# A listed prologue and a modulation with stationary weights, in a two-layer hybrid mixer on one core

## The chip, the cores and the metric

The kernel runs on one core of a Trainium2 chip. The metric is the time of one execution on the device in microseconds; the time given is the median of several runs.

## The reference, cut to what matters

Two layers work on 1024 latent tokens and 256 context tokens of 1024 channels. Each layer begins with a modulated norm, then one input projection, three head groups (Fourier mixing, pooling, differential attention), gates, an output projection and a gated residual. The diff touches only the beginning of the first layer:

```
shift, scale, gate     = split(silu(c)     @ w_mod + b_mod, 3)
shift_c, scale_c, gate_c = split(silu(c_ctx) @ w_mod + b_mod, 3)
h  = rms_norm(x,   norm_g) * (1 + scale)   + shift
hc = rms_norm(ctx, norm_g) * (1 + scale_c) + shift_c
p  = h @ w_in          # and hc @ w_in
```

`shift` and `scale` have one value for each of the 1024 channels, for the latent tokens and for the context.

## The kernel before, in words

Each engine carries out its instructions in the order in which the program lists them. Transfers are queued on SP, in their listed order too; a tile of a pool waits for a free buffer. The pool `big` (tag `t5`) has 28 buffers, PSUM 8 banks (`PX`) in this phase.

*Layout.* Tokens come in ten tiles `xn[0]` to `xn[9]` of 128 tokens (8 latent, 2 context), in three groups `g`: tiles 0 to 3, 4 to 7, 8 and 9. Channels come in eight tiles `k` of 128. The projection wants the channels on the partitions: `h_block(l, k, g, ...)` transposes the tiles of a group for channel tile k on TensorE (L280), multiplies by the scale and adds the shift out of PSUM (L284 on ScalarE or L286 on VectorE), copies that into a rounded part (L287, ScalarE) and subtracts to get the remainder (L289, POOL, for group 2 VectorE). `proj_T_k` (L340) then runs, for each of two output halves, three matmuls (rounded by rounded, remainder by rounded, rounded by remainder) into one PSUM bank for each half and group (`psg`). The split of a weight chunk into its two parts is `w_split` (L317, L318).

*Modulation.* Shift and scale of layer 0 come in four quarters of two channel tiles each. A quarter's weights are four transfers of 512 KB (`mod0_load`, L147). For quarters 0 to 2 `mod0_mm` (L156) holds `sc[:, k, :]` (128x2, silu of the two conditioning vectors) stationary and streams 512 columns of weights; the 2x512 result is copied to a row (L161), transposed in four pieces (L165) and finished by four small VectorE operations (`mod_finish`, L135 to L140). Quarter 3 is multiplied and accumulated on VectorE (`mod0_acc`, L175 and L177, 32 operations of 256 columns), summed over the partitions on TensorE (`mod0_sum`, L186, eight matmuls) and finished likewise.

*Norm.* `rms` squares a tile in two halves on ScalarE (L266) and takes three small POOL operations for the reciprocal root (L267 to L269); `norm` multiplies on VectorE (L581).

*Order.* The queue on SP carries quarters 0 to 2, the first weight chunk (two transfers of 512 KB), ten token tiles, quarter 3 and the next chunk. TensorE does the three quarters, then a loop over 24 items (k, g), first k = 0 to 5 for group 0, 1, 2, then k = 6 and 7, for which quarter 3 is needed. Item n's `hb` is listed before the matmuls `gk` of item n - 3; norms, the eight steps `next(acc)` of quarter 3 and its sum hang on chosen items.

Of the kernel before, what the change touches and what calls it, by code (L numbers as in the profile page):

```python
# [18 lines left out]
D = 1024  # L19
# [12 lines left out]
def build(tc, I, out):  # L32
# [13 lines left out]
    def nm(s):  # L46
        cnt[0] += 1
        return f"{s}_{cnt[0]}"
# [4 lines left out]
    def E2(shape=(128, 512), dt=F32):  # L53
        return e2p.tile(list(shape), dt, tag="e2", name=nm("e2"))

    def SM(n=1, dt=F32):
        return smp.tile([128, n], dt, tag=f"sm{n}", name=nm("sm"), bufs={1: 16, 4: 14}.get(n, 4))
# [9 lines left out]
    def PX(dt=F32, n=512):  # L67
        return PSP["pool"].tile([128, n], dt, tag="x", name=nm("x"))
# [60 lines left out]
    def mod_finish(l, k, sh, scl):  # L129

        n = sh.shape[1]

        def cols(t, o):
            return t[:, l, o + k:o + k + n].unsqueeze(2).to_broadcast([128, n, 2])
        dve.tensor_tensor(shiftT[l][:, k:k + n, :], sh, cols(bmodT, 0), ADD)  # L135
        t = SM(16)
        tv = t.rearrange("p (k t) -> p k t", t=2)[:, 0:n, :]
        dve.tensor_tensor(tv, scl, cols(bmodT, 8), ADD)
        dve.tensor_scalar(tv, tv, 1.0, None, ADD)
        dve.tensor_tensor(scaleT[l][:, k:k + n, :], tv, cols(ngT, 0), MULT)  # L140
# [7 lines left out]
            ws.append(w)  # L148
        return ws

    def mod0_mm(ws, half_way=None):
        ps = PX()
        for k in range(KT):
            if k == KT // 2 and half_way:
                half_way()
            pe.matmul(ps[0:2, :], lhsT=sc[:, k, :], rhs=ws[k // 2][:, k % 2, :], start=(k == 0), stop=(k == KT - 1))  # L156
        return ps

    def mod0_fin(q, pm):
        row = E2()  # L160
        dve.tensor_copy(row[0:2, :], pm[0:2, :])  # L161
        ps = PX()
        psv = ps[:, 0:8].rearrange("p (i c t) -> p i c t", i=2, c=2)
        for i in range(4):
            pe.transpose(ps[:, 2 * i:2 * i + 2], row[0:2, i * 128:i * 128 + 128], ident[0:2, 0:2])  # L165
        mod_finish(0, 2 * q, psv[:, 0], psv[:, 1])

    def mod0_acc(ws, acc):
        for k in range(KT):
# [7 lines left out]
                        dve.scalar_tensor_tensor(a, w, sk, a, MULT, ADD)  # L177
            yield

    def mod0_sum(q, acc):  # L180
        ps = PX()
        psv = ps[:, 0:8].rearrange("p (i c t) -> p i c t", i=2, c=2)
        for i in range(2):
            for ct in range(2):
                for t in range(2):
                    pe.matmul(psv[:, i, ct, t:t + 1], lhsT=acc[:, 2 * i + t, ct * 128:ct * 128 + 128],  # L186
                              rhs=ones[:, 0:1], start=True, stop=True)
        mod_finish(0, 2 * q, psv[:, 0], psv[:, 1])

    def mod_acc(src, c0, sides, res, lead=1):  # L190

# [67 lines left out]
    def x_rms(x, r):  # L259

        ss = SM(2)
        for hf in range(2):
            if hf:
                yield
            sq = E2()
            act.activation(sq, x[:, hf * 512:hf * 512 + 512], AF.Square, accum_out=ss[:, hf:hf + 1])  # L266
        pool.tensor_tensor(r, ss[:, 0:1], ss[:, 1:2], ADD)  # L267
        pool.tensor_scalar(r, r, 1.0 / D, EPS, MULT, ADD)
        pool.tensor_tensor(r, r, mhalf[:, 0:1], ALU.pow)  # L269

    GROUPS = {0: (0, 1, 2, 3), 1: (4, 5, 6, 7), 2: (8, 9)}

    def h_block(l, k, g, xn, H, on_act=False):
        tiles = GROUPS[g]
        s = 1 if g == 2 else 0
        n = 128 * len(tiles)
        c0 = tiles[0] * 128
        ps = PX()
        for i, j in enumerate(tiles):
            pe.transpose(ps[:, i * 128:i * 128 + 128], xn[j][:, k * 128:k * 128 + 128], ident)  # L280
        hf = E2()
        sc1, sh1 = scaleT[l][:, k, s:s + 1], shiftT[l][:, k, s:s + 1]
        if on_act:
            act.activation(hf[:, :n], ps[:, :n], AF.Identity, scale=sc1, bias=sh1)  # L284
        else:
            dve.tensor_scalar(hf[:, :n], ps[:, :n], sc1, sh1, MULT, ADD)  # L286
        act.activation(H[k][0][:, c0:c0 + n], hf[:, :n], AF.Copy)  # L287
        eng = dve if g == 2 else pool
        eng.tensor_tensor(H[k][1][:, c0:c0 + n], hf[:, :n], H[k][0][:, c0:c0 + n].bitcast(F32), SUB)  # L289


    wsrc = []
# [245 lines left out]
    def layer(l, src, dst, carry):  # L538
# [23 lines left out]
        def newH(k):  # L562
            if H[k] is None:
                H[k] = [T5([128, NTOK], F32R) for _ in range(2)]

        if full:
            xn, rx = {}, {}

            def x_in(*js):
                for j in js:  # L570
                    xn[j] = x_load(src, j)

            def rms(*js):
                for j in js:
                    rx[j] = SM(1)
                    for _ in x_rms(xn[j], rx[j]):
                        pass

            def norm(*js):
                for j in js:  # L580
                    dve.tensor_scalar(xn[j], xn[j], rx[j], None, MULT)  # L581

            def hb(k, g, on_act):
                newH(k)
                h_block(l, k, g, xn, H, on_act)

            def gk(k, *gs):
                for ct in range(2):
                    proj_T_k(psg[ct], H, W, ct, ntokA, k, gs)

            wm = [mod0_load(q) for q in range(3)]
            w_dma()
            x_in(0, 1, 2, 3, 4, 5, 6, 7, 8, 9)
            ms = [mod0_mm(wm[0])]
            ms.append(mod0_mm(wm[1], lambda: mod0_fin(0, ms[0])))
            ms.append(mod0_mm(wm[2], lambda: mod0_fin(1, ms[1])))
            w_split()
            W = wready.pop(0)
            a3 = T5([128, 4, 256])
            psg = [[PX() for _ in cols(ntokA)] for _ in range(2)]  # L600
            items = [(k, g) for g in (0, 1, 2) for k in range(6)] + [(k, g) for k in (6, 7) for g in (0, 1, 2)]
            at = {n: [] for n in range(len(items))}
            at[0] += [lambda: rms(0, 1, 2, 3), lambda: norm(0, 1), lambda: mod0_fin(2, ms[2]), lambda: norm(2, 3)]
            for n, j in enumerate((4, 5, 6, 7, 8, 9)):
                at[n] += [lambda j=j: rms(j)]
                at[n + 1] += [lambda j=j: norm(j)]
            for n in range(8, 16):
                at[n] += [lambda: next(acc)]
            at[18] += [lambda: mod0_sum(3, a3)]
            for n in range(len(items) + 3):  # L610
                if n < len(items):
                    for f in at[n]:
                        f()
                    hb(*items[n], 6 <= n < 17)
                if n == 0:
                    w3 = mod0_load(3)
                    acc = mod0_acc(w3, a3)
                    w_dma()
                if n >= 3:
                    gk(*items[n - 3])  # L620
                if n == 20:
                    pool.tensor_scalar(pscT, pscT, 0.5, 0.0, MULT, ADD)
                    tabs = fourier_tabs(l)
                    css = [fourier_load(l, ct) for ct in range(2)]
                if n == 22:
                    w_split()
                    w_dma()
        else:
            xn, tail = carry
            k = 0  # L630
            for n in range(14):
                next(tail)
                if n in (4, 5, 6, 8, 9, 11, 12, 13):
                    newH(k)
                    h_block(l, k, 0, xn, H)
                    k += 1
            W = wready.pop(0)
            for k in range(k, KT):
                newH(k)
                h_block(l, k, 0, xn, H)  # L640
            psg = [[PX() for _ in cols(ntokA)] for _ in range(2)]
            hb = iter(range(KT))
            for k in range(KT):
                if k >= KT - 1:
                    h_block(l, next(hb), 1, xn, H)
                for ct in range(2):
                    proj_T_k(psg[ct], H, W, ct, ntokA, k, (0,))
                if k in (0, 1, 3, 7):
                    next(tail, None)
                if k == 1:  # L650
                    w_split()
                    w_dma()
                if k == 7:
                    css = [fourier_load(l, ct) for ct in range(2)]
            for k in range(-2, KT + 0):
                if (h := next(hb, None)) is not None:
                    h_block(l, h, 1, xn, H)
                if 0 <= k < KT:
                    for ct in range(2):
                        proj_T_k(psg[ct], H, W, ct, ntokA, k, (1,))  # L660
                if 0 <= k - 0 < KT:
                    h_block(l, k - 0, 2, xn, H)
# [698 lines left out]
```

## Time and profile before

| | us |
|---|---|
| median of 3 runs | 1412.21 (1408.42 to 1413.48) |
| the profiled execution's own time | 1411.95 |
| its span, first to last instruction | 1410.2 |
| TensorE busy in the span | 1345.6 (95%) |
| VectorE, POOL, ScalarE busy | 852.9, 799.1, 540.5 |

PE is TensorE's matmuls, PEld its weight loads, DVE VectorE, ACT ScalarE, POOL GpSimd, SP the queue of transfers. Times in rows are microseconds from the start of the span. A number with an x counts records; an f32 matmul leaves two records of each kind, a transpose one.

### The profile page before, as it was taken

The page shows a single profiled execution, that of the slowest core. Times are in us where ns is not written, and L with a number is a line of the kernel's source. Part 1 is how long each engine was busy: PE and PEld are TensorE (multiplying, and loading weights), DVE is VectorE, ACT ScalarE, POOL GpSimd, SP SyncE. Part 2 cuts the span into 40 slices and gives each one's busy share as a digit, 9 for nine tenths or more (in the row PEclk, how much of TensorE's full clock was granted, in tenths as well). Part 3 has the DMA queues.
Part 4 walks back from the last instruction along what each step waited for, and adds up shares of the span by engine and source line. Part 5 has one row for each costly group of instructions (what it writes and reads, how often), then busy time and mean ns, then how long its engine had stood idle before and what let it go on. Part 6 is the DMA issues. An engine that isn't in the chain of part 4 may idle for free.

```text
span 1410.2 us, 24603 instructions
## 1 busy us (share of the span) xinstructions
PE 1345.6 (95%) x9780; PEld 1206.5 (86%) x9780; DVE 852.9 (60%) x1274; ACT 540.5 (38%) x1152; POOL 799.1 (57%) x867
## 2 busy tenths in 40 slices
PE   7899999999999988999998899999999998899998
PEld 1688899889999977889997678898999996799997
DVE  2854366795975057677775554464365216878784
ACT  2632213111211156676664332221122216666662
POOL 2633216766574057788875732326676306777773
PEclk9989999999999999999999999999999999999999
DMA  9321152692232013021221221536402201111211
GB/s 357 121 82 34 40 192 87 233 321 81 73 126 87 1 62 119 20 79 52 95 101 63 101 68 34 207 90 216 155 31 82 91 2 50 57 46 46 91 38 61
DMA packets 64867, 137.11 MB, mean 97 GB/s; under 512 B 7280, under 2 KB 19184, under 8 KB 64752
## 3 DMA queue, kind: packets, MB, share of 16 engines
q1 hardware_dynamic: 54608, 118.26, 24.8%
q10 hardware_dynamic: 10144, 17.28, 3.6%
q8 instruction: 77, 1.26, 0.4%
q14 instruction: 38, 0.31, 0.1%
HBM read 105.63 MB, written 29.88 MB: 96 GB/s over the span
## 4 chain that ended last, share of the span: by engine, by line
PE 80%; DVE 7%; ACT 5%; POOL 3%; issue 3%; DMA 2%; SPq 0%; DVEq 0%; POOLq 0%; ACTq 0%
PE x L360 30%; PE x L340 12%; PE S L917 9%; PE x L997 8%; PE x L1055 7%; PE x L750 4%; ACT t L941 3%; PE x L981 3%; PE x L156 1%; DVE t L212 1%; DVE sm L926 1%; PE x L894 1%; PE x L433 1%; POOL t L289 1%; DVE t L177 1%
## 5 line engine op out<-in xcount | busy, mean ns | idle before, releaser
L360 PE MATMUL x<-wh,t 128*128 128x256 f32 x2432 | 448.5, 285 | 0.0
L360 PEld LDWEIGHTS x<-wh,t 128*128 128x128 f32 x2432 | 382.2, 192 | 1.8 <-issue 1.0
L360 PE MATMUL x<-wl,t 128*128 128x256 f32 x1216 | 344.4, 283 | 0.0
L926 DVE TENSOR_REDUCE sm<-S 128x1 f32<-128x1280 f32 (+1 forms) x132 | 189.6, 1478 | 151.0 <-PE S L917 151.0
L360 PEld LDWEIGHTS x<-wl,t 128*128 128x128 f32 x1216 | 233.6, 192 | 1.3 <-issue 1.2
L941 ACT ACTIVATE t<-S,sm 128x1280 f32<-128x1280 f32 (+1 forms) x140 | 172.6, 1238 | 85.0 <-DVE sm L926 82.1
L340 PE MATMUL x<-t,wh 128*128 128x512 f32 (+1 forms) x640 | 173.8, 382 | 9.5 <-DVE t L289 4.6
L997 PE MATMUL x<-t,t 128*128 128x128 f32 x1312 | 163.3, 280 | 4.2 <-DVE t L984 4.0
L997 PEld LDWEIGHTS x<-t,t 128*128 128x128 f32 x1312 | 154.0, 194 | 9.2 <-DVE t L984 4.2
L917 PE MATMUL S<-t,e 64*128 64x512 f32 (+1 forms) x1152 | 131.7, 370 | 13.8 <-ACT t L986 12.8
L340 PEld LDWEIGHTS x<-t,wh 128*128 128x128 f32 x640 | 114.2, 192 | 32.9 <-POOL t L289 5.8
L917 PEld LDWEIGHTS S<-t,e 64*128 64x128 f32 x1152 | 100.8, 188 | 44.3 <-ACT t L986 24.8
L318 POOL TENSOR_TENSOR wl<-st,wh 128x1024 fp32r<-128x1024 f32 x32 | 83.0, 2592 | 79.5 <-ACT wh L317 79.3
L964 POOL TENSOR_TENSOR t<-t,t 128x768 f32<-128x768 f32 (+1 forms) x64 | 115.0, 1797 | 5.3
L317 ACT ACTIVATE wh<-st 128x1024 fp32r<-128x1024 f32 x64 | 65.1, 1064 | 107.9 <-PE x L750 70.2
L1055 PE MATMUL x<-wh,e 128*128 128x256 f32 (+1 forms) x456 | 103.8, 309 | 2.3 <-ACT e L1037 2.1
L340 PE MATMUL x<-t,wl 128*128 128x512 f32 (+1 forms) x320 | 100.4, 375 | 1.3 <-DVE wl L318 1.3
L750 PE MATMUL x<-wh,t 128*128 128x512 f32 x288 | 89.3, 390 | 0.0
L212 DVE SCALAR_TENSOR_TENSOR t<-t,sc,t 128x512 f32<-128x512 f32 x98 | 86.2, 920 | 3.6 <-DMA t<-in_wmB_dram 3.2
L981 PE MATMUL x<-ident,t 128*128 128x128 f32 x520 | 80.9, 278 | 2.8 <-ACT t L986 1.4
L1055 PEld LDWEIGHTS x<-wh,e 128*128 128x128 f32 x456 | 76.9, 192 | 5.9 <-ACT e L1037 2.5
L1059 POOL TENSOR_TENSOR t<-e,t 128x256 f32<-128x256 f32 (+1 forms) x60 | 47.5, 792 | 56.3 <-DVE e L1058 56.3
(229 smaller groups left out, 2269.1 us busy)
## 6 DMA issues: line engine op xcount, KB each, us to landing
st<-in_w_in_dram SPq DMA_DIRECT2D x48, 512.0 KB, 4.6
t<-in_wmB_dram ACTq DMA_DIRECT2D x24, 512.0 KB, 5.7
xpart<-e SPq DMA_DIRECT2D x36, 256.0 KB, 4.0
t<-xpart SPq DMA_DIRECT2D x18, 512.0 KB, 4.4
t<-in_wmS_dram SPq DMA_DIRECT2D x16, 512.0 KB, 8.3
st<-in_w_out_dram SPq DMA_DIRECT2D x16, 512.0 KB, 4.3
t<-in_x_dram SPq DMA_DIRECT2D x10, 512.0 KB, 10.3
e<-in_x_dram SPq DMA_DIRECT2D x20, 256.0 KB, 5.2
```

Of the source, the lines that this page charges most:

```text
L212: dve.scalar_tensor_tensor(a, w, sk, a, MULT, ADD)
L318: lo_eng[hf].tensor_tensor(lo[:, sl, :], st, hi[:, sl, :].bitcast(F32), SUB)
L340: pe.matmul(p[:, :m], lhsT=W[wi][:, k, ct * 128:ct * 128 + 128], rhs=H[k][hi][:, c0:c0 + m], start=(n == 0), stop=(n == 3 * KT - 1))
L360: pe.matmul(bank[:, i * 256:i * 256 + 256], lhsT=H[k][hi][:, j * 128:j * 128 + 128], rhs=W[wi][:, k, :], start=(n == 0), stop=(n == 3 * KT ...
L750: pe.matmul(ps, lhsT=zr[k][zi][:, j * 128:j * 128 + 128], rhs=W[wi][:, k, :], start=(k == 0 and n == 0), stop=(k == 3 and n == 2))
L917: pe.matmul(S[m][:, i * nk + c:i * nk + c + w], lhsT=Q[q][r, h * 128:h * 128 + 128], rhs=k[h][r, k0 + c:k0 + c + w], start=(n == 0), stop= ...
L926: dve.tensor_reduce(nb, S[:, :nh * nk].rearrange("p (h k) -> p h k", h=nh), AX.X, ALU.min)
L941: act.activation(p[:, sl], S[:, sl], AF.Exp, bias=nb[:, i:i + 1], scale=-1.0, accum_out=ls[:, i:i + 1])
L964: pool.tensor_tensor(p[0][:, cut:end], p[0][:, cut:end], p[1][:, cut:end], ADD)
L981: pe.transpose(ps[:, i * 128:i * 128 + 128], s["p"][0][:, (t0 + i) * 128:(t0 + i + 1) * 128], ident)
L997: pe.matmul(o[:, i * 128:i * 128 + 128], lhsT=s["PT"][:, i * nkt + t, :], rhs=vv[h][:, kt0 + t, :], start=(t == 0), stop=(t == nkt - 1))
L1055: pe.matmul(ps[:, :m], lhsT=s["z"][zi][:, k * 128:k * 128 + 128], rhs=Wa[hf][wi][:, k, w0:w0 + m], start=(n == 0), stop=(n == 11))
```

## The change

- Transfers are queued in another order: tokens 0 to 3, quarter 0, the weight chunk, quarter 1, tokens 4 to 7, quarter 2, tokens 8 and 9, quarter 3. The next weight chunk follows once the first is split.
- `mod0_mm` holds 128x128 pieces of the modulation weights stationary and streams `sc[:, k, :]` (two columns): 32 matmuls a quarter, whose results lie by channel. Quarter 0 runs k outside, in four banks; the others run one output piece after the other. The row copy and its transposes go; quarter 0 is finished by two calls of `mod_finish`.
- The reciprocal root is taken for two token tiles at once: two small VectorE operations and one on POOL.
- `h_block` is divided into `h_trans` and `h_split`; here all remainders go to POOL, and group 2, and group 1 from k = 4, take their first step on ScalarE.
- The loop over items is replaced by a written list. `m`, `f`: a quarter's matmuls and its finish; `n`: norm of two tiles; `t k g`: transposes; `s k g`: the split; `g k g`: the projection matmuls; `P`, `Q`: the two halves of the first weight split, rounded parts on ScalarE and remainders on VectorE; `a`: one step of quarter 3 on VectorE; `d`: its sum; `X`: table loads; `Y`: the next split.

```
+    def mod0_mm(q, ws):
+        banks = [PX() for _ in range(4 if q == 0 else 1)]
+        if q == 0:
+            ps = [b[:, 0:2] for b in banks]
+            order = [(k, c) for k in range(KT) for c in range(4)]
+        else:
+            ps = [banks[0][:, 2 * c:2 * c + 2] for c in range(4)]
+            order = [(k, c) for c in range(4) for k in range(KT)]
+        for k, c in order:
+            pe.matmul(ps[c], lhsT=ws[k // 2][:, k % 2, c * 128:c * 128 + 128], rhs=sc[:, k, :], start=(k == 0), stop=(k == KT - 1))
+        return banks
...
+    def h_split(l, k, g, ps, H, on_act=False, lo_eng=None):
...
+        eng = lo_eng or (dve if g == 2 else pool)
...
+                    h_split(l, *a, banks[a], H, a[1] == 2 or (a[0] >= 4 and a[1] == 1), pool)
...
+            x_in(0, 1, 2, 3)
+            wm = [mod0_load(0)]
             w_dma()
+            wm.append(mod0_load(1))
+            x_in(4, 5, 6, 7)
+            wm.append(mod0_load(2))
+            x_in(8, 9)
+            wm.append(mod0_load(3))
...
+                    "m0 n01 n23 t00 t10 t20 t30 f0 P s00 s10 Q g00 g10 m1 n45 n67 f1 s20 s30 t01 t11 t21 t31 s01 s11 m2 s21 s31 n89",
+                    "f2 g20 g30 t40 t50 s40 s50 a a a t41 t51 s41 s51 a a a g01 g11 g21 g31 t02 t12 s02 s12 a a g40 g50 t22 t32 s22 s32",
+                    "g41 g51 t42 s42 t52 s52 t60 t70 X d f3 s60 s70 g02 g12 g22 g32 t61 t71 s61 s71 g42 g52 Y g60 g70 t62 t72 s62 s72",
+                    "g61 g71 g62 g72"):
```

## Rows read from the trace of the kernel before

**Rows 1.** The page: busy time of the engines over the span, and the shares of the chain that ended last.

```profile
PE 1345.6 (95%) x9780; PEld 1206.5 (86%) x9780; DVE 852.9 (60%) x1274; ACT 540.5 (38%) x1152; POOL 799.1 (57%) x867
PE 80%; DVE 7%; ACT 5%; POOL 3%; issue 3%; DMA 2%; SPq 0%; DVEq 0%; POOLq 0%; ACTq 0%
```

**Rows 2.** Windows of all engines: the stretch, its length, busy time and records of PE, PEld, DVE, ACT and POOL, the granted clock (1.00 is 2.4 GHz), the DMA engines' busy share and GB/s.

```profile
0.00:92.00 92.00, 74.03 (x309) 45.71 (x309) 50.71 (x90) 40.09 (x91) 39.72 (x53) 0.93 0.56 202
92.00:1411.00 1319.00, 1271.54 (x9472) 1160.83 (x9472) 802.20 (x1184) 500.37 (x1063) 759.39 (x814) 0.99 0.27 90
```

**Rows 3.** The chain that ended last, from 0 to 140 us: its shares by line, and pieces with start, length and the line they lie on.

```profile
by line: PE x L340 35.1%; PE x L156 14.5%; DVE t L177 7.2%; issue 5.6%; DVE t L175 3.7%; POOL t L289 3.0%; DVE t L581 2.8%; DMA t<-in_wmS_dram 2.8%; DVE e L286 2.7%; PE x L433 2.6%; PE x L280 2.4%; PE x L186 2.3%; ACT t L287 2.1%; DVE t L28
...
71.88 3.21 PE x L186 x16
...
89.23 0.86 PE x L340 x5
...
91.93 28.12 PE x L340 x144
```

**Rows 4.** TensorE's instructions in order of time: start, length, line, operation, output and inputs, shape, count, and the idle time before with what ended it.

```profile
18.78 7.03 PE L156 MATMUL x<-t,sc 128*2 128x512 f32 x16
25.74 0.40 PE L165 MATMUL x<-ident,e 2*128 2x2 f32 x4
...
66.61 0.39 PE L340 MATMUL x<-t,wh 128*128 128x256 f32 x1 [2.40 <-DVE t L289]
...
71.68 3.41 PE L186 MATMUL x<-ones,t 128*128 128x1 f32 x16
74.95 1.09 PE L280 MATMUL x<-ident,t 128*128 128x128 f32 x4
...
77.12 1.05 PE L280 MATMUL x<-ident,t 128*128 128x128 f32 x4
77.83 0.78 PE L340 MATMUL x<-t,wh 128*128 128x256 f32 x2
...
79.40 0.48 PE L340 MATMUL x<-t,wh 128*128 128x256 f32 x2
...
80.19 0.60 PE L280 MATMUL x<-ident,t 128*128 128x128 f32 x4
80.55 0.71 PE L340 MATMUL x<-t,wh 128*128 128x512 f32 x2
...
82.02 0.60 PE L280 MATMUL x<-ident,t 128*128 128x128 f32 x4
```

**Rows 5.** VectorE's instructions in order of time, columns as in the group before.

```profile
18.89 0.16 DVE L135 TENSOR_TENSOR shiftT<-x,bmodT 128x4 f32<-128x4 f32 x1 [3.09 <-PE x L165]
...
19.36 0.16 DVE L140 TENSOR_TENSOR scaleT<-sm,ngT 128x4 f32<-128x4 f32 x1
22.41 0.68 DVE L161 COPY e<-x 2x512 f32<-2x512 f32 x1 [2.89 <-PE x L156]
...
36.79 0.81 DVE L286 TENSOR_SCALAR e<-x,scaleT,shiftT 128x512 f32<-128x512 f32 x1
...
42.10 0.75 DVE L581 TENSOR_SCALAR t<-t,sm 128x1024 f32<-128x1024 f32 x1 [0.28 <-POOL sm L269]
...
52.53 5.27 DVE L175 TENSOR_SCALAR t<-t,sc 128x256 f32<-128x256 f32 x4
...
66.48 1.66 DVE L177 SCALAR_TENSOR_TENSOR t<-t,sc,t 128x256 f32<-128x256 f32 x4
```

**Rows 6.** Windows of TensorE: the stretch, its length, busy time and records, the granted clock, the DMA engines' busy share and GB/s.

```profile
4.00:10.90 6.90, 5.71 (x7) 1.00 1.01 329
10.90:29.70 18.80, 18.77 (x50) 1.00 1.04 401
29.70:34.90 5.20, 1.11 (x8) 1.00 1.02 408
34.90:38.30 3.40, 3.40 (x15) 0.50 1.04 391
...
69.00:71.70 2.70, 2.47 (x13) 0.50 0.48 124
71.70:75.10 3.40, 3.40 (x18) 0.50 0.38 122
75.10:79.26 4.16, 4.16 (x21) 0.50 0.16 47
79.26:90.00 10.74, 9.52 (x56) 1.00 0.16 51
```

**Rows 7.** The first users of the first and of the thirteenth transfer of 512 KB, in TensorE's and ScalarE's order of time; in brackets the wait that the landing ended.

```profile
5.19 13.32 PE L156 MATMUL x<-t,sc 128*2 128x512 f32 x24 [5.19 <-DMA t<-in_wmS_dram]
...
22.66 1.06 ACT L317 ACTIVATE wh<-st 128x1024 fp32r<-128x1024 f32 x1 [19.76 <-DMA st<-in_w_in_dram]
```

**Rows 8.** ScalarE's and POOL's instructions in order of time.

```profile
36.25 0.63 ACT L287 ACTIVATE t<-e 128x512 fp32r<-128x512 f32 x1 [4.50 <-DVE e L286]
36.78 0.61 ACT L266 ACTIVATE e<-t 128x512 f32<-128x512 f32 x1
...
28.93 0.56 POOL L269 TENSOR_TENSOR sm<-sm,mhalf 128x1 f32<-128x1 f32 x1
...
39.27 1.28 POOL L289 TENSOR_TENSOR t<-e,t 128x512 fp32r<-128x512 f32 x1
...
86.18 2.71 POOL L318 TENSOR_TENSOR wl<-st,wh 128x1024 fp32r<-128x1024 f32 x1 [0.60 <-ACT wh L317]
```

More of the change, by code (lines that the diff above doesn't have):

```diff
@@ L149, in mod0_load, with mod0_fin @@
         return ws
[L151 to L166, printed above, removed]
+    def mod0_mm(q, ws):
[9 more added lines that the diff above has]
+        return banks
+    def mod0_fin(q, banks):
+        if q == 0:
+            v = [b[:, 0:2].rearrange("p (c t) -> p c t", c=1) for b in banks]
+            for ct in range(2):
+                mod_finish(0, ct, v[ct], v[2 + ct])
+        else:
+            v = banks[0][:, 0:8].rearrange("p (i c t) -> p i c t", i=2, c=2)
+            mod_finish(0, 2 * q, v[:, 0], v[:, 1])
     def mod0_acc(ws, acc):
@@ L185, in mod0_sum @@
                 for t in range(2):
-                    pe.matmul(psv[:, i, ct, t:t + 1], lhsT=acc[:, 2 * i + t, ct * 128:ct * 128 + 128],
+                    o = 4 * i + 2 * ct + t
+                    pe.matmul(ps[:, o:o + 1], lhsT=acc[:, 2 * i + t, ct * 128:ct * 128 + 128],
                               rhs=ones[:, 0:1], start=True, stop=True)
-        mod_finish(0, 2 * q, psv[:, 0], psv[:, 1])
+        return [ps]
     def mod_acc(src, c0, sides, res, lead=1):
@@ L271, in build, with h_trans @@
     GROUPS = {0: (0, 1, 2, 3), 1: (4, 5, 6, 7), 2: (8, 9)}
-    def h_block(l, k, g, xn, H, on_act=False):
-        tiles = GROUPS[g]
-        s = 1 if g == 2 else 0
[L276 to L280, printed above, removed]
+    def h_trans(k, g, xn):
+        ps = PX()
+        for i, j in enumerate(GROUPS[g]):
+            pe.transpose(ps[:, i * 128:i * 128 + 128], xn[j][:, k * 128:k * 128 + 128], ident)
+        return ps
+    def h_split(l, k, g, ps, H, on_act=False, lo_eng=None):
+        s = 1 if g == 2 else 0
+        n = 128 * len(GROUPS[g])
+        c0 = GROUPS[g][0] * 128
         hf = E2()
@@ L287, in h_block @@
         act.activation(H[k][0][:, c0:c0 + n], hf[:, :n], AF.Copy)
-        eng = dve if g == 2 else pool
+        eng = lo_eng or (dve if g == 2 else pool)
         eng.tensor_tensor(H[k][1][:, c0:c0 + n], hf[:, :n], H[k][0][:, c0:c0 + n].bitcast(F32), SUB)
+    def h_block(l, k, g, xn, H, on_act=False):
+        h_split(l, k, g, h_trans(k, g, xn), H, on_act)
     wsrc = []
@@ L573, in rms @@
             def rms(*js):
[L574 to L589, printed above, removed]
@@ L591, in layer @@
-            wm = [mod0_load(q) for q in range(3)]
-            w_dma()
[L593 to L598, printed above, removed]
-            a3 = T5([128, 4, 256])
-            psg = [[PX() for _ in cols(ntokA)] for _ in range(2)]
-            items = [(k, g) for g in (0, 1, 2) for k in range(6)] + [(k, g) for k in (6, 7) for g in (0, 1, 2)]
@@ L602, in layer @@
[L602 to L627, printed above, removed]
+                ss, r = SM(4), SM(4)
@@ new lines, in rms @@
+                for i, j in enumerate(js):
+                    for hf in range(2):
+                        sq = E2()
+                        act.activation(sq, xn[j][:, hf * 512:hf * 512 + 512], AF.Square,
+                                       accum_out=ss[:, 2 * i + hf:2 * i + hf + 1])
+                r = r[:, 0:2]
+                dve.tensor_tensor(r, ss[:, 0:4:2], ss[:, 1:4:2], ADD)
+                dve.tensor_scalar(r, r, 1.0 / D, EPS, MULT, ADD)
+                pool.tensor_tensor(r, r, mhalf[:, 0:2], ALU.pow)
@@ new lines, in rms, with norm, run @@
+                return r
+            def norm(js, r):
+                for i, j in enumerate(js):
+                    dve.tensor_scalar(xn[j], xn[j], r[:, i:i + 1], None, MULT)
+            psg = [[None] * len(cols(ntokA)) for _ in range(2)]
+            banks, mods = {}, {}
+            def run(op, *a):
+                if op == "m":
+                    mods[a[0]] = mod0_mm(a[0], wm[a[0]])
+                elif op == "f":
+                    mod0_fin(a[0], mods[a[0]])
+                elif op == "n":
+                    norm(a, rms(*a))
+                elif op == "t":
+                    banks[a] = h_trans(*a, xn)
+                elif op == "s":
+                    newH(a[0])
+                    h_split(l, *a, banks[a], H, a[1] == 2 or (a[0] >= 4 and a[1] == 1), pool)
+                elif op == "g":
+                    k, g = a
+                    for ct in range(2):
+                        if psg[ct][g] is None:
+                            psg[ct][g] = PX()
+                        proj_T_k(psg[ct], H, W, ct, ntokA, k, (g,))
@@ new lines, in layer @@
+            x_in(0, 1, 2, 3)
+            wm = [mod0_load(0)]
+            w_dma()
+            wm.append(mod0_load(1))
[3 more added lines that the diff above has]
+            wm.append(mod0_load(3))
+            a3 = T5([128, 4, 256])
+            acc = mod0_acc(wm[3], a3)
+            for text in (
[4 rows of a table added]
+                for op in text.split():
+                    if op == "P":
+                        (sts, a, b), W = wst.pop(0), [wp.tile([128, 8, 256], F32R, tag=t, name=nm(t)) for t in ("wh", "wl")]
+                        for hf, part in enumerate(sts):
+                            act.activation(W[0][:, 4 * hf:4 * hf + 4, :], part, AF.Copy)
+                    elif op == "Q":
+                        for hf, part in enumerate(sts):
+                            sl = slice(4 * hf, 4 * hf + 4)
+                            dve.tensor_tensor(W[1][:, sl, :], part, W[0][:, sl, :].bitcast(F32), SUB)
+                        w_dma()
+                    elif op == "a":
+                        next(acc)
+                    elif op == "d":
+                        mods[3] = mod0_sum(a3)
+                    elif op == "X":
+                        pool.tensor_scalar(pscT, pscT, 0.5, 0.0, MULT, ADD)
+                        tabs = fourier_tabs(l)
+                        css = [fourier_load(l, ct) for ct in range(2)]
+                    elif op == "Y":
+                        w_split()
+                        w_dma()
+                    else:
+                        run(op[0], *map(int, op[1:]))
```

3 lines of the change are left out of this document (1 added, 2 removed).

## The prediction, made before the change was run

> **What bounds the kernel now.** I read the page's busy shares and its chain first [rows 1]: TensorE is busy 95% of the span, and 80% of the chain that ended last lies on it. So a microsecond counts only where TensorE waits or runs at its low clock. The windows say where that is [rows 2]: in the first 92 us, all that the diff touches, TensorE is busy 74.0 us, at a mean granted clock of 0.93; in the 1319 us behind it waits only 47 us. What is gained or lost ahead of 92 us is thus passed on nearly one to one.
>
> The chain of those 92 us [rows 3] runs over the modulation matmuls (L156), later over VectorE's accumulation of the last quarter (L175, L177), then over the sum of that accumulation on TensorE (L186, from 71.88), then over the blocks k = 6 and 7, to 90.09. Behind a short wait the next projection starts at 91.93. The number to move is the start of L186, and then the 18.2 us from there to 90.09.
>
> **Prices.** A modulation quarter costs TensorE 7.0 us now (16 records of L156) plus 0.40 us for four small transposes, and 0.68 us of VectorE for the row copy [rows 4, 5]. The new form, 128x128 f32 weights under two moving columns, does not occur. Its nearest row is L186: the same weights under one column, two records for each matmul, 16 records from 71.68 to 74.95, so 0.204 us a record [rows 4]. A quarter has 32 matmuls, 64 records: 13.1 us at that rate. But L186 ran at a granted clock of 0.50, the 1.2 GHz level [rows 6]. At the high level no such row exists. The transposes load f32 weights of that shape too; four take 0.71 us at the low clock (77.12 to 77.83) and 0.36 at the high one (80.19 to 80.55) [rows 4]. Scaled in that way a record takes 0.10 us and a quarter 6.5 us. So the bounds of a quarter are 6.5 and 13.1 us, and the clock decides between them.
>
> **The clock, as the rows have it.** In the first stretch the profile shows 1.00, but 7 records in 5.71 us is the low rate against 0.43 us a record later: L156 itself began low, at 5.19, and was high from about 10.9, 5.7 us later [rows 6]. The clock fell at 34.9, 5.2 us after L156 had ended; it rose at 38.3, after 3.4 us of unbroken transposes and projection; it fell at 69.0, after TensorE had idled 2.4 us, from 64.2 to 66.61, and had only short runs behind that; and it rose at 79.26 [rows 4, 6]. In 71.7 to 75.1 TensorE was busy all of 3.40 us, nearly all with L186, yet the clock stayed low, and rose only 4.2 us after the dense work behind it began. So I read L186, and with it the new matmuls, as work that does not lift the clock.
>
> The Trainium skill, "TensorE: Matmul & The Clock Gate", section on the HAM clock gate, says that sustained matmul activity releases the throttle and that time counts, not a number of matmuls; by that the first quarter would lift the clock for the rest, which is the first rival below, and the stretch of L186 speaks against it. Its section "LDWEIGHTS (loading the stationary operand)" gives columns divided by 1.2, an estimate of 107 ns for a 128-column load and 6.8 us a quarter at any clock; L186 took 204 ns, so the measurement goes first.
>
> **The walk along TensorE's new order.** Loads: the first 512 KB landed at 5.19 and the thirteenth at 22.66, or 1.46 us each [rows 7]; `wm[0]` is now the fifth to eighth, so TensorE starts at 11.0 instead of 5.19, from the low state.
> - `m0`, 64 records at 0.204: 13.1, to 24.1. It is not bound by loads (1.46 us for 16 records).
> - `t00` to `t30`, 16 transposes at the low rate, 0.18 to 0.21 each (0.18 above; the second figure from 15 records in 3.40 us of the stretch from 34.9 [rows 6], which holds two longer ones): 3.2, to 27.3. The tokens are long ready: x3 lands at about 9.6; two squares (0.6 each), the power (0.56) and two norms (0.75 each) [rows 5, 8] end near 14.
> - `f0` is eight small operations in place of four: twice 0.63 [rows 5], to 25.4. `s00`, `s10`: 0.81 on VectorE, 0.6 on ScalarE, 1.3 on POOL, in a pipeline [rows 5, 8]; the second remainder is there at 29.5, and the five matmuls of `g10` behind it end at about 30.7. The clock rises meanwhile.
> - `m1` from 30.7: high until the clock falls, about 5.0 us later (5.2 in the first fall, 4.8 from the start of the idling in the second), which is 50 records; 14 more at 0.204 make 2.9: to 38.6. Bounds 6.5 and 13.1.
> - `t01` to `t31`, low: 3.2, to 41.8. x4 to x7 land by about 30 and are normed by 36, under `m1`.
> - `m2`: 3.2 us of transposes is less than the 3.4, 4.2 and 5.7 us that preceded the rises, so low throughout: 13.1, to 54.9. If the clock rises just before, 8 us.
> - `g20`, `g30`: 12 matmuls of 512 columns, 0.45 low (twice the 256-column 0.237 less a little) and 0.245 high [rows 4]; the rise comes 4.2 us in: 4.9, to 59.8. `t40`, `t50`: 0.7, to 60.5.
> - VectorE does `s40`, `s50` (0.81 each) by 61.7, and only then the 32 operations `a`; between them stands no other VectorE work. Before, L175 took 1.32 us each beside POOL's L289, and L177 0.415 alone [rows 5]. POOL has four L289 of 512 columns (`s40` to `s51`) at the same point, so I take 5.3 + 28 x 0.415 = 16.9, to 78.6. From below 13 us (L175 at 0.35), from above 18.
> - Meanwhile TensorE has 48 matmuls of 512 columns and 28 transposes up to `t70`, 14.3 us, ending at 74.8, and waits for `d` until 78.6, against 71.88 before: **6.7 us late**.
> - From `d` on: 16 records at the low clock, 3.3; then 48 matmuls of 256 columns (0.13), 24 of 512 and 12 transposes (0.09), 13.2 us at the high rates [rows 4]. As after L186 before, 4.2 us of it pass at the low clock and do 2.1 of work; POOL's queue, with `Y`'s 2.7 us ahead of the last two remainders [rows 8], adds about 0.6. Sum 19.3 against 18.2: **1.1 late**.
>
> The row copies, the four small transposes and TensorE's idling around 30 us are gone; comparing 78.6 with 71.88 contains that. The sum is +7.8. I put +7, since `m2` may catch part of a rise, and that can only shorten it.
>
> **Edits costed at nothing.** The SP queue issues the same 30 loads of 512 KB. `wm[3]` stands behind x8 and x9 and lands by about 44 (27 steps of 1.46 behind 5.19), 17 us before `a`; if `m` were quick, 2 us before. The norm's two additions go from POOL to VectorE, 0.2 us each, under `m0`. The first remainder of W, 1.2 us more on VectorE and 2.4 less on POOL, lies under `t30` and `g00`. The remainders of group 2 go to POOL (0.7 each) and its first step to ScalarE, both with slack while VectorE accumulates; without that cover `a` would be 3 us longer. `X` issues the same seven table loads, needed at 90. PSUM has eight banks; `m0` with `t00` to `t30` fills them, and `g00` waits for `s00`, counted above.
>
> The same page of the Trainium skill, "Part 4: PE-mode transpose", says that transposes do not lift the clock. Here it rose at 38.3 after 3.4 us that were mostly transposes, so the row decides; by the page `g00` and `g10` would stay low and end 1 to 2 us later.
>
> **Rivals.**
> 1. *Faster: the quarters at the high rate*, 6.5 us each. Then `m0` ends by its last load, about 17; `m1` 24.2 (its last load) with 30.7 at the end; `t01` waits for the norm of x7 until 33; `m2` ends at 41.2, `t50` at 44.8, `s50` at 46, `a` at 63, 9 us ahead of 71.88. With 16 to 19 us from there: -8 to -12, about 1402. For it: scaling with the clock, as transposes do. Against it: TensorE idles until 11 and starts low, and L186 did not lift the clock. Between the two a record of about 0.15 us would leave the time unchanged.
> 2. *Half of it:* `m0` low, but transposes and blocks lift the clock for most of `m1` and `m2` (6.5 and 8). That is 6 us less than my walk: 1413, no change.
> 3. *Low throughout*: `m1` 13.1, `g`-blocks 0.45 each and `a` at 18: +5 to +9 on the walk, about 1426. For it: the second fall came after idling of only 3 us; against it: 3.4 us lifted the clock at 38.3.
>
> **How the numbers follow.** The profiled execution took 1411.95 us (span 1410.2), 0.26 below the median; +7 makes 1419. Its own range is 1415 to 1423. Chances: the walk 0.53, rival 1 0.15, rival 2 0.20, rival 3 0.12. What can be told from no change is 0.5%, 7 us, or 1419.3, right at the forecast, so half of the walk's chance counts as slower: in round figures faster 0.15, the same 0.45, slower 0.40. The range takes in rival 2, the middle of 3 and the near half of 1: 1402 to 1426.
>
> **What would show it.** L156's successor in 64 records of 0.20 us from 11 to 24; a granted clock of 0.50 in most of `m2`; VectorE's L175 beginning at about 62; the sum of the last quarter at about 79; the last L340 of the first projection at about 97 instead of 90. Records of 0.10 us, or the sum before 70, would make it wrong.

## The result and the profile after

The changed kernel took a median of 1427.55 us (1427.00 to 1430.16, four runs) beside 1411.49 us of the kernel before on the same chip: a ratio of 1.0129 (95% interval 1.0110 to 1.0148; the quotient of the two medians is 1.0114), so 16 us slower, where +7 had been forecast and 1426 was the upper end. The profiled execution took 1427.0 us, span 1425.2. One execution of the kernel before, beside e9 and e10 below, took 2156.4 us at a mean granted clock of 0.56 and is left out of its median.

The page's busy shares of the kernel after, which answer [rows 1]: TensorE is busy 11 us more, VectorE and ScalarE as before.

```profile
PE 1356.8 (95%) x9912; PEld 1240.7 (87%) x9912; DVE 851.4 (60%) x1277; ACT 540.0 (38%) x1153; POOL 793.1 (56%) x849
```

Windows of all engines after, cut where the first projection has ended and the next begins (106.4, against 92 in [rows 2]). The mean clock ahead of the cut is 0.84 where it was 0.93; the stretch behind it is as long as before (1319.6 against 1319.0).

```profile
0.00:106.40 106.40, 85.82 (x441) 79.82 (x441) 47.77 (x93) 40.07 (x92) 35.25 (x35) 0.84 0.49 175
106.40:1426.00 1319.60, 1270.94 (x9472) 1160.89 (x9472) 803.65 (x1184) 499.93 (x1063) 757.86 (x814) 0.99 0.27 90
```

The chain that ended last, after (start, length, engine and line, records); L162 is the new modulation matmul, L192 the sum of quarter 3, L351 the projection. The sum starts at 85.02 instead of 71.88, the next projection at 106.36 instead of 91.93 [rows 3]: 14.4 us, all of it ahead of that point.

```profile
34.62 11.81 PE x L162 x64
...
49.96 10.35 PE x L162 x64
60.30 4.47 PE x L351 x12
...
66.78 4.17 DVE t L181 x4
...
85.02 3.54 PE x L192 x16
...
102.93 1.58 PE x L351 x11
...
106.36 28.12 PE x L351 x144
```

TensorE's instructions after, in order of time, columns as in [rows 4]. A quarter of 64 records took 13.8, 12.0 and 10.6 us where the old form took 7.0 at the high level [rows 4]; two waits on POOL stand before `m1`, and one of 5.25 us before the sum.

```profile
12.22 13.79 PE L162 MATMUL x<-sc,t 128*128 128x2 f32 x64 [12.22 <-DMA t<-in_wmS_dram]
...
30.98 0.50 PE L351 MATMUL x<-t,wh 128*128 128x512 f32 x1 [1.19 <-POOL t L297]
...
33.20 0.50 PE L351 MATMUL x<-t,wh 128*128 128x512 f32 x1 [0.57 <-POOL t L297]
...
34.46 11.98 PE L162 MATMUL x<-sc,t 128*128 128x2 f32 x64
...
49.75 10.55 PE L162 MATMUL x<-sc,t 128*128 128x2 f32 x64
...
85.02 3.54 PE L192 MATMUL x<-ones,t 128*128 128x1 f32 x16 [5.25 <-DVE t L183]
```

Windows of TensorE after, columns as in [rows 6]. It is busy without a gap from 34.4 to 63.2, yet the clock falls in the middle of `m1` (0.88 in the mean of 34.4 to 36.9 puts the fall at 36.3), is high for 3.4 us from 50.0 and falls again in the middle of `m2`. In the first row 64 records took 13.7 us, 0.21 each, under a clock shown as 1.00; records at the high level take about half of that (32 in 3.40 us, fourth row).

```profile
12.20:25.90 13.70, 13.68 (x65) 1.00 1.05 401
34.40:36.90 2.50, 2.50 (x21) 0.88 1.02 392
36.90:50.00 13.10, 13.10 (x64) 0.50 0.55 207
50.00:53.40 3.40, 3.40 (x32) 0.99 0.01 2
53.40:63.20 9.80, 9.80 (x40) 0.50 0.10 29
```

### The profile page after: what moved, and what is told of

The parts are those of the page before. It is cut to its first block, busy times and chain, and to the rows that moved or that the text cites. A ratio compares the mean times of both kernels' runs of the same rounds, so it can differ in the third digit from the quotient of the medians.

```text
span 1425.2 us, 24857 instructions
## 1 busy us (share of the span) xinstructions
PE 1356.8 (95%) x9912; PEld 1240.7 (87%) x9912; DVE 851.4 (60%) x1277; ACT 540.0 (38%) x1153; POOL 793.1 (56%) x849
## 3 DMA queue, kind: packets, MB, share of 16 engines
q8 instruction: 78, 1.28, 0.4%
## 4 chain that ended last, share of the span: by engine, by line
PE 79%; DVE 6%; ACT 5%; POOL 4%; issue 3%; DMA 3%; SPq 0%; DVEq 0%; POOLq 0%; ACTq 0%
PE x L371 29%; PE x L351 12%; PE S L952 9%; PE x L1032 8%; PE x L1090 6%; PE x L785 4%; PE x L1016 3%; ACT t L976 3%; PE x L162 2%; DMA e<-in_x_dram 1%; PE x L929 1%; DVE sm L961 1%; POOL t L297 1%; PE x L444 1%; DVE t L218 1%
## 5 line engine op out<-in xcount | busy, mean ns | idle before, releaser
L351 PE MATMUL x<-t,wh 128*128 128x512 f32 (+1 forms) x640 | 172.2, 381 | 5.1 <-POOL t L297 3.7
L952 PE MATMUL S<-t,e 64*128 64x512 f32 (+1 forms) x1152 | 132.5, 370 | 13.1 <-ACT t L1021 12.5
L351 PEld LDWEIGHTS x<-t,wh 128*128 128x128 f32 x640 | 115.5, 194 | 27.2 <-POOL t L297 5.4
L351 PE MATMUL x<-t,wl 128*128 128x512 f32 (+1 forms) x320 | 101.1, 377 | 1.3 <-DVE wl L329 1.3
L218 DVE SCALAR_TENSOR_TENSOR t<-t,sc,t 128x512 f32<-128x512 f32 x98 | 91.6, 979 | 3.4 <-DMA t<-in_wmB_dram 3.0
L297 POOL TENSOR_TENSOR t<-e,t 128x512 fp32r<-128x512 f32 (+1 forms) x40 | 49.5, 1256 | 68.4 <-ACT t L295 68.3
```

The lines of the kernel that those rows point to most:

```text
L351: pe.matmul(p[:, :m], lhsT=W[wi][:, k, ct * 128:ct * 128 + 128], rhs=H[k][hi][:, c0:c0 + m], start=(n == 0), stop=(n == 3 * KT - 1))
L952: pe.matmul(S[m][:, i * nk + c:i * nk + c + w], lhsT=Q[q][r, h * 128:h * 128 + 128], rhs=k[h][r, k0 + c:k0 + c + w], start=(n == 0), stop= ...
```

## The experiments

After the result the theory (A in the expectations) was that of the prediction: 128x128 f32 weights under two columns keep TensorE at its low level, or take it there. Against it stood that the order of the list costs the time, whatever the form of the matmuls.

All medians, each beside the kernel before on the same chip in the same session. "Sum" is the start of the last quarter's sum, "next" the start of the next projection, both in us of the profiled execution; the last column is the median less "next", the part that the diff doesn't touch.

| kernel | median | before | ratio (95%) | sum | next | rest |
|---|---|---|---|---|---|---|
| before | 1411.49 | | | 71.88 | 91.93 | 1319.6 |
| after | 1427.55 | 1411.49 | 1.0129 (1.0110 to 1.0148) | 85.02 | 106.36 | 1321.2 |
| e1_old_form | 1420.14 | 1408.79 | 1.0076 (1.0051 to 1.0102) | 79.67 | 100.94 | 1319.2 |
| e2_wide | 1414.58 | 1408.79 | 1.0039 (1.0022 to 1.0055) | 72.42 | 92.83 | 1321.8 |
| e3_q_early | 1424.60 | 1408.79 | 1.0108 (1.0061 to 1.0155) | 81.17 | 102.62 | 1322.0 |
| e4_before_new_form | 1422.94 | 1408.79 | 1.0099 (1.0064 to 1.0133) | 85.37 | 102.21 | 1320.7 |
| e5_wide_q_early | 1408.95 | 1409.84 | 1.0007 (0.9986 to 1.0028) | 68.51 | 88.89 | 1320.1 |
| e6_wide_all_pe | 1412.74 | 1409.84 | 1.0015 (1.0000 to 1.0029) | none | 89.45 | 1323.3 |
| e7_pool_free | 1429.11 | 1409.84 | 1.0146 (1.0122 to 1.0169) | 83.25 | 104.20 | 1324.9 |
| e8_quarter_first | 1412.29 | 1409.84 | 1.0019 (1.0000 to 1.0037) | none | 93.27 | 1319.0 |
| e9_list_mended | 1405.87 | 1410.21 | 0.9964 (0.9948 to 0.9981) | none | 85.12 | 1320.8 |
| e10_two_columns | 1424.70 | 1410.21 | 1.0110 (1.0080 to 1.0141) | none | 104.22 | 1320.5 |

The prologue moves by 21 us between the kernels and the rest by 6: a microsecond ahead of the next projection is passed on, as the prediction took it, to within about 3 us.

### The new form alone, in the kernel before (e4)

The order, the loads and the last quarter are those of the kernel before; the three quarters on TensorE are multiplied as in the kernel after.

```
-            pe.matmul(ps[0:2, :], lhsT=sc[:, k, :], rhs=ws[k // 2][:, k % 2, :], ...)
+            pe.matmul(ps[c], lhsT=ws[k // 2][:, k % 2, c * 128:c * 128 + 128], rhs=sc[:, k, :], ...)
```

> The kernel before, in its own order, with only the form of the three TensorE quarters changed to the new one (128x128 weights stationary, two columns streamed). Theory A: all three quarters at the low clock from 5.2 on, 13 us each, so the first projection matmul moves from 37.6 to about 49, time 1421 to 1425. Theory B (the form does not matter): 1410 to 1414.

The chain of e4:

```profile
5.21 41.10 PE x L162 x192
...
85.37 1.71 PE x L192 x16
```

Windows of TensorE in e4, the same stretch:

```profile
5.20:46.30 41.10, 41.09 (x193) 1.00 0.96 363
```

192 records in 41.10 us: 0.214 each over 41 us without a gap, the low rate of L186 (0.204). Nothing waits in that stretch, so the form alone does it. The sum of the last quarter, one moving column, ran at the high level in e4: 16 records in 1.71 us, 0.107 each, where they took 0.204 before. So the low price is the clock's and not the shape's. The next projection is 10.3 us late, the median 1.0% longer.

The Trainium skill, "TensorE: Matmul & The Clock Gate", section "What's actually happening", says that activity of the engine releases the throttle. Here it did not in 41 us, in which the engine was busy 41.09 us. Its section "Seeing it yourself" warns that the clock events of a trace have been observed to be unreliable and that a single one is not fully to be trusted. The trace agrees: the window shows 1.00 while the records ran at the low rate.

### More columns for the same weights (e2, e5)

e2 is the kernel after with the two conditioning columns repeated to 128; 126 of the 128 result columns are left unread.

```
+    scw = T5([128, KT, 128])
+    dve.tensor_copy(scw.rearrange("p k (e t) -> p k e t", t=2), sc.unsqueeze(2).to_broadcast([128, KT, 64, 2]))
...
-            pe.matmul(ps[c], ..., rhs=sc[:, k, :], ...)
+            pe.matmul(pw[c], ..., rhs=scw[:, k, :], ...)
```

> The changed kernel, but each modulation matmul streams 128 columns (the two columns repeated 64 times) past the same stationary weights; 64 times the columns, the same count of matmuls and weight loads. Theory A (clock): the wider matmuls lift the clock, records of about 0.11 us, 7 us a quarter, the sum of the last quarter near 70, time about 1413: more work in less time. Theory C (a 128x128 f32 weight load costs 0.2 us at any clock): records stay at 0.20 us or more, time 1427 or more. Theory B (order): within 2 us of the changed kernel, 1427.

TensorE's instructions in e2:

```profile
15.08 8.90 PE L164 MATMUL x<-t,t 128*128 128x128 f32 x64 [15.08 <-DMA t<-in_wmS_dram]
...
32.77 7.31 PE L164 MATMUL x<-t,t 128*128 128x128 f32 x64
...
41.66 7.39 PE L164 MATMUL x<-t,t 128*128 128x128 f32 x64
```

Windows of TensorE in e2, most of `m1`:

```profile
32.80:40.00 7.20, 7.20 (x66) 1.00 1.04 393
```

With 64 times the columns the quarters took 8.9, 7.3 and 7.4 us instead of 13.8, 12.0 and 10.6. `m1` and `m2` ran at a clock that stays high: 0.11 us a record, near the 0.10 that the prediction had scaled from the transposes. `m0` begins low, as after, but 8.9 us is well below the 13.7 of 64 low records, so the clock rose on the way. The sum starts 12.6 us earlier than after, and the ratio falls from 1.0129 to 1.0039. That settles the theory: same weights, list and loads, more work, less time. e2 lost 2.9 us at its start: by the profile the load of quarter 0 was issued only once a small transfer ahead of it had landed. In e5, whose loads are the same, that wait is 1.6 us and `m0` starts at 12.9, so the loss belongs to the execution and not to the form. SP's waits in e2 (total, times, longest):

```profile
SPq L149 <- DMA bmodT<-in_bmodT_dram: 3.7, 1, 3.7
```

e5 adds to e2 the move of e3 (below): 1408.95 us, the time of the kernel before.

> The changed kernel with the 128-column modulation matmuls and with the remainders of the first weight chunk ahead of the finish of quarter 0 (the second and third experiments together); quarter 3 still on VectorE. If the two losses are separate, their gains add: the sum of the last quarter, at 85.0 in the changed kernel, 72.4 with the wide form and 81.2 with the early remainders, starts at 66 to 69; the time is that of the kernel before within 3 us. If both gain the same wait, the sum stays at 71 or later and the time 5 us above the kernel before.

The sum of e5 is 3.4 us ahead of that of the kernel before, its next projection 3.0; the median shows no difference that its interval can tell.

### The old form in the new list (e1)

> The changed kernel with its new order of loads and its written list, but the three TensorE quarters of the modulation in the form of before (two stationary columns, 512 streamed, row copy, four small transposes). Theory A (the two-column form keeps TensorE at its low clock and costs 10 to 14 us a quarter): quarters of about 6.9 us once the clock is high, the sum of the last quarter starts near 70 instead of 85.0, time about 1413. Theory B (the new order, with the last quarter in one VectorE stretch, is what costs): the sum starts at 82 or later, time 1424 or more.

```
-            pe.matmul(ps[c], lhsT=ws[k // 2][:, k % 2, c * 128:c * 128 + 128], rhs=sc[:, k, :], ...)
+            pe.matmul(ps[0:2, :], lhsT=sc[:, k, :], rhs=ws[k // 2][:, k % 2, :], ...)
```

It came out 7 us above what A had expected: A alone was too simple, the list has a price of its own under the old form. VectorE's instructions in e1:

```profile
52.53 1.42 DVE L595 TENSOR_SCALAR t<-t,sm 128x1024 f32<-128x1024 f32 x2 [0.81 <-POOL sm L590]
53.86 0.67 DVE L163 COPY e<-x 2x512 f32<-2x512 f32 x1
```

TensorE in e1, the small transposes that follow that copy:

```profile
54.59 0.52 PE L167 MATMUL x<-ident,e 2*128 2x2 f32 x4 [3.77 <-DVE e L163]
```

The list has `n89` between `m2` and `f2`. For the new form this costs nothing, since `f2` reads PSUM at once. For the old form the row copy (L163) stands on VectorE behind the norm of tokens 8 and 9 (L595), TensorE idles 3.77 us, and the clock falls: 0.59 in the mean of 54 to 58. Before `m1` TensorE waits 4.0 us, 2.2 of them on ScalarE and 1.8 on POOL, where after it waits 1.8. So e1 is 9.0 us late at "next" by the list and the order of the loads, which no run took apart, e4 10.3 by the form, after 14.4 by both, and e2, with this list and high quarters, 0.9: the costs neither add nor belong to one part alone.

### The first weight split earlier (e3)

```
-"m0 n01 n23 t00 t10 t20 t30 f0 P s00 s10 Q g00 ...
+"m0 n01 n23 P Q t00 t10 t20 t30 f0 s00 s10 g00 ...
```

> The changed kernel with the remainders of the first weight chunk (two VectorE operations, 3.42 us beside POOL) listed ahead of the finish of quarter 0, where VectorE idles. If that wait is on the path: the first projection blocks end near 32 instead of 34.6, time about 1425. If the clock gives it back (quarter 1 then falls to the low clock at the same moment with less done before): 1427, no change.

In the kernel after, the two remainders of W (L648, VectorE) run at the same time as POOL's two remainders of the tokens (L297), for which `g00` and `g10` wait. VectorE after:

```profile
28.58 3.42 DVE L648 TENSOR_TENSOR wl<-st,wh 128x1024 fp32r<-128x1024 f32 x2
```

POOL after, the same microseconds:

```profile
28.55 4.59 POOL L297 TENSOR_TENSOR t<-e,t 128x512 fp32r<-128x512 f32 x2 [15.27 <-ACT t L295]
```

VectorE in e3, where POOL is idle at that point:

```profile
18.26 2.52 DVE L648 TENSOR_TENSOR wl<-st,wh 128x1024 fp32r<-128x1024 f32 x2 [3.81 <-ACT wh L644]
```

Each slows the other: 1.71 us for one L648 beside POOL, 1.26 alone; 2.30 for one remainder of POOL beside VectorE, 1.28 alone [rows 8]. The two remainders thus came 2.0 us later than two at 1.28 would have, which covers the two waits before `m1` (1.76 in all). Which of the two loses more varies: in e7 below, where this stretch is listed as after, L648 takes 2.28 us and the remainder 1.75. In e3 TensorE passes from `t30` to the end of `m2` without a wait, `m1` takes 10.2 us, and the next projection starts 3.7 us earlier. The clock falls in `m1` (at 36.1) and in `m2` all the same, so the waits before `m1` are not what takes it. The gain is shown by the trace alone: the intervals of the two ratios overlap.

The Trainium skill, "GPSIMD Engine Reference", section "1. Specifications", says that GpSimd shares its way to SBUF with VectorE, with contention where VectorE reads two inputs from there. L648 does, and the trace agrees with these figures.

### POOL kept out of the stretch on VectorE (e7)

The four remainders that run beside the accumulation go to VectorE, ahead of it.

```
-..., pool)
+..., dve if a[0] in (4, 5) and a[1] < 2 else pool)
...
-f2 g20 g30 t40 t50 s40 s50 a a a t41 t51 s41 s51 a a a g01 ...
+f2 g20 g30 t40 t50 t41 t51 s40 s50 s41 s51 a a a a a a g01 ...
```

> The changed kernel, but the remainders of the four 512-column blocks beside the VectorE stretch (k = 4 and 5, groups 0 and 1) go to VectorE ahead of the stretch, so that POOL is idle at its start. If VectorE's slow operations (1.0 us each instead of 0.35 for the first four, and gaps after them) come from POOL working beside them, the stretch shrinks from 18.1 to about 13.5 us and the four remainders cost 3 of that back: the sum starts 1 to 2 us earlier, time about 1426. If POOL does not matter, the stretch stays at 18 and the sum starts 3 us later, time about 1430.

VectorE after (L181 is the first product of each of four sums, L183 the multiply-and-add):

```profile
66.70 4.25 DVE L181 TENSOR_SCALAR t<-t,sc 128x256 f32<-128x256 f32 x4
...
70.87 15.18 DVE L183 SCALAR_TENSOR_TENSOR t<-t,sc,t 128x256 f32<-128x256 f32 x28
```

VectorE in e7:

```profile
69.21 1.13 DVE L181 TENSOR_SCALAR t<-t,sc 128x256 f32<-128x256 f32 x4
...
70.26 14.03 DVE L183 SCALAR_TENSOR_TENSOR t<-t,sc,t 128x256 f32<-128x256 f32 x28
```

The mechanism was there: L181 took 0.28 us instead of 1.06, and the stretch 13.9 us instead of 18.1. The gain was not: the four splits, now ahead of the stretch with their remainders on VectorE, waited in turn for ScalarE's rounded parts, so that from the start of `s40` to the start of the stretch 6.9 us went by instead of 1.5. The chain of e7:

```profile
33.35 9.91 PE x L162 x64
...
57.10 4.74 PE x L351 x12
...
83.25 3.55 PE x L192 x16
```

From the start of `g20` to the sum e7 takes 26.2 us, the kernel after 24.7. The sum does start 1.8 us earlier than after, as expected, but that is luck: `m1` began 1.3 us earlier and took 1.9 us less, ahead of all that the edit touches, since the clock fell later in it. The median was no lower than after's.

### The last quarter on TensorE too (e6, e8)

e6 takes the 128 columns for all four quarters and a list of its own; VectorE accumulates nothing, and `d` and the `a` are gone.

```
-            acc = mod0_acc(wm[3], a3)
...
+"m0 n01 n23 P Q t00 t10 t20 t30 f0 s00 s10 g00 g10 m1 n45 n67 f1 s20 s30 t01 t11 t21 t31 s01 s11 m2 s21 s31 f2",
+"g20 g30 t40 t50 s40 s50 n89 t41 t51 s41 s51 g01 g11 t02 t12 s02 s12 g21 g31 m3 t60 t70 f3 s60 s70 t22 t32 s22 s32",
...
```

> As the fifth experiment, but quarter 3 also runs on TensorE in the 128-column form, with no accumulation on VectorE, and the list is rearranged around it. Theory: TensorE, kept at its high clock, needs 7 us for a quarter that costs VectorE 18 and TensorE a wait and a low clock; TensorE runs without a wait from about 30 us on, the first projection ends near 80 instead of 90.0 (before) and 104.3 (changed), the time is 8 to 10 us below the kernel before. Rival: POOL's remainders (24 of them) become the limit of the blocks and the end stays at 88 or later, the time within 3 us of the kernel before.

A gain of 8 to 10 us had been expected and none came. TensorE's transposes in e6 (L287):

```profile
53.61 0.45 PE L287 MATMUL x<-ident,t 128*128 128x128 f32 x1 [2.75 <-DVE t L604]
...
55.19 0.90 PE L287 MATMUL x<-ident,t 128*128 128x128 f32 x3 [1.14 <-DVE t L604]
```

`n89` had been listed behind the splits, so the norm of tokens 8 and 9 (L604) came late for `t02` and `t12`: 3.9 us of waits, and the projection behind them ran at the low level, 4.5 us for 12 matmuls against 2.8 elsewhere. e8 loads quarter 0 ahead of the tokens.

> As the sixth experiment, but quarter 0 of the modulation is loaded ahead of the tokens instead of behind them. TensorE then starts near 5.2 instead of 12, but the first norm is 5 us later. If loading the tokens first is worth something, this is slower than the sixth by 1 to 4 us; if TensorE's start counts, faster by 2 to 5.

Its next projection starts 3.8 us later than that of e6, yet the medians agree (1412.29 and 1412.74). That the two profiled executions differ behind this point by 6.8 us the other way (span less "next" 1315.2 in e8, 1322.0 in e6) shows how far a single profile reaches: a few microseconds behind the prologue come and go between executions (the ten of e6 took 1407.9 to 1414.3).

### The list mended, and the same with two columns (e9, e10)

e9 is e6 with `n89` ahead of `f2`; e10 is e9 with the two columns of the kernel after.

```
-... m2 s21 s31 f2", "g20 g30 t40 t50 s40 s50 n89 t41 ...
+... m2 s21 s31 n89 f2", "g20 g30 t40 t50 s40 s50 t41 ...
```

> The sixth experiment (all four quarters on TensorE, 128 columns, early remainders) with the norm of tokens 8 and 9 listed before the finish of quarter 2 again, since there TensorE waited 3.9 us for that norm (50.5 to 55.2) and then ran low until 59.7. Theory: TensorE runs without a longer wait from 24.7 on, the first projection ends near 80 instead of 87.4, the next one starts near 82 (91.93 in the kernel before), and the time is 6 to 10 us below the kernel before. Rival: what is gained in the first 90 us is lost behind it, as the sixth experiment seemed to show (2.5 us earlier at its next projection, yet 2.9 us longer in the median): then the time stays within 3 us of the kernel before.

> The ninth experiment with one thing changed back: the modulation matmuls stream two columns instead of 128; weights, count, order and list are the same. Theory (clock): four quarters of 10 to 13.6 us instead of 7 to 8.8, so the next projection starts 12 to 22 us later than in the ninth and the time is longer by as much, though TensorE streams 64 times fewer columns. Rival (the form does not matter once VectorE's stretch is gone): within 3 us of the ninth.

TensorE's quarters in e9:

```profile
12.39 8.87 PE L164 MATMUL x<-t,t 128*128 128x128 f32 x64 [12.39 <-DMA t<-in_wmS_dram]
...
29.45 7.31 PE L164 MATMUL x<-t,t 128*128 128x128 f32 x64
...
38.34 7.40 PE L164 MATMUL x<-t,t 128*128 128x128 f32 x64
...
56.07 7.30 PE L164 MATMUL x<-t,t 128*128 128x128 f32 x64
```

TensorE's quarters in e10:

```profile
11.47 13.79 PE L162 MATMUL x<-sc,t 128*128 128x2 f32 x64 [11.47 <-DMA t<-in_wmS_dram]
...
32.52 9.05 PE L162 MATMUL x<-sc,t 128*128 128x2 f32 x64
...
44.65 10.77 PE L162 MATMUL x<-sc,t 128*128 128x2 f32 x64
...
68.71 10.91 PE L162 MATMUL x<-sc,t 128*128 128x2 f32 x64
```

Side by side in one session, the column count alone makes 18.8 us: 44.5 us for four quarters at two columns, 30.9 at 128, the rest in the transposes and projections that then run at the low level. e9 beats both kernels, with a median of 1405.87 us against 1410.21 before. It fell short of the 6 to 10 us expected: 4.3, and its next projection starts 6.8 us ahead of that of the kernel before.

## Why the prediction was off

The direction and the mechanism were right: slower, since the new matmuls run at the low level and do not lift it (e4, e2 against after, e10 against e9). The size was half of what came. The walk of the prediction beside the trace, each row the length of a step:

| step | put, us | measured | difference |
|---|---|---|---|
| start of `m0` | 11.0 | 12.2 | +1.2 |
| `m0` | 13.1 | 13.65 | +0.55 |
| `t00` to `t30` | 3.2 | 3.3 | +0.1 |
| `g00`, `g10` | 3.4 | 5.3 | +1.9 |
| `m1` | 7.9 | 11.8 | +3.9 |
| `t01` to `t31` | 3.2 | 3.45 | +0.25 |
| `m2` | 13.1 | 10.4 | -2.7 |
| `g20`, `g30` | 4.9 | 4.45 | -0.45 |
| to the end of `s50` | 1.9 | 2.2 | +0.3 |
| the stretch `a`, to the sum | 16.9 | 18.2 | +1.3 |
| sum to the last projection matmul | 19.3 | 19.3 | 0 |

The sum is +6.4 on a forecast of +7.8. That makes 14.2, and the trace has 14.4 at the next projection; the other 1.6 us of the median lie behind that point, no more than single profiles differ there.

- **The step that failed is the term for `m1`.** It put 50 records at the high rate and 14 low; the trace has about 17 high and the rest low, 11.8 us, near the upper bound of 13.1 that the prediction named. The 5.0 us had been read from two falls behind an idle TensorE [rows 6] and carried over to a TensorE that is busy with few columns. There the clock fell 1.8 us into `m1` after, 3.8 in e3, 3.9 in e7 and 5.0 in e10. No row of before bore that carrying over, and what sets the moment is not shown.
- **`g00` and `g10`** waited because VectorE's L648 and POOL's L297 share their time. The prediction said that the first remainder of W "lies under `t30` and `g00`"; it did, but it slowed the remainders that `g00` and `g10` wait for (e3). The same mechanism had been read for L175 beside POOL, and costed only there.
- **`m2`** caught a rise that the prediction had named as possible: high from 50.0 to 53.4. This gave 2.7 us back, which is luck: without it the forecast would have been further off.
- **The stretch `a`** came out at its upper bound, 18: four L181 took 4.25 us, less than the 5.3 put for L175, but L183 took 0.54 us each where the 0.415 of a VectorE alone had been taken. The prediction had moved the remainders of group 2 to POOL at no cost; they run beside L183. In e7 they are all that is left of POOL there, up to 78.5: the chain has 8 of L183 in 4.37 us from 70.66, while they run, and 8 in 3.25 us from 79.87, behind them. That is a reading of the trace; no run took them away alone.
- **The other edits costed at nothing** cost nothing from there on: from 34.4 to the end of `s50` TensorE waits for nothing, so neither the loads nor the norms nor the finishes stand in its way.
- **The tail** was right to the tenth, but by errors that cancel: the clock stayed low for some 9.3 us from the start of the sum, where 7.5 had been put, and the blocks behind it took 10.0 us instead of 11.8, some 0.9 less than the longer low stretch explains. The prices of a record were near, at the low rate (0.213 for 0.204) and at the high one (0.11 for 0.10, e2).
- **Rival 3** gave the number, 1426, not the course: it had `m1` and `m2` low throughout, and they were partly high. Rival 1 had the price right and the clock wrong: e5 and e2 show what the quarters at the high rate are worth. That rival put the sum at 63 and the time at 1402; e5 has 68.5 and 1409, with quarters of 9.7, 7.3 and 7.4 us instead of 6.5.

The range ended at 1426 because the upper bounds of single terms (`m1` 13.1, `a` 18, the blocks low) had been put into a rival at 0.12 as if they came only together; `m1` and `a` were near theirs although the rest was not.

What stays open: why `m0` began 1.2 us later than the landings of before gave; why, behind the prologue, e6 and e7 take some 3 us more than the others; when the clock falls in a quarter of two columns; and what a count of columns between 2 and 128 would do, which no run tried.

## What to carry to other kernels

With the same weights to load, a record cost much the same with 1, 2 and 128 moving columns: 0.107, 0.106 and 0.114 us at the high level (e4, after, e2), and twice that at the low one. What differed was the clock that the matmul left to itself and its neighbours. So look for a row of that shape at either level, and where only the low level has one, cost the work around it low as well, as the upper bound. Filling the columns with copies can be cheaper than leaving them out (18.8 us, e9 and e10). In an order written by hand, the small operations on which TensorE waits (a norm, a copy, a remainder) decide as much as the matmuls: the place of `n89` is the one difference between e6 and e9, and 4.3 us at the next projection. VectorE and POOL, which slowed each other here, are to be costed as slowed wherever they meet, not only where the old trace showed it.

## What was unexpected of the hardware

- The clock shown can be 1.00 while the records run at the low rate: 41 us in e4, 13.7 us after, both ahead of the first change in the trace. The rate of like records is the safer reading there.
- A fully busy TensorE lost its clock twice under two columns (after, 36.3 and 53.4) and kept it through the quarters of 128 (e2, e9).
- By the profile, the load of quarter 0 waited for `bmodT`, a small transfer that it doesn't read: 3.7 us in e2, 1.6 in e5, 1.1 after.
